# A 2-layer encoder trunk on one core: the input also comes transposed from the host, and the first norm drops its transposes

## The chip, the cores and the metric

The kernel runs on one core of a Trainium2 chip. A core has five engines, each working through its own list of instructions in order: TensorE (PE, matrix products, with PEld for its weight loads), VectorE (DVE), ScalarE (ACT), GpSimd (POOL) and SyncE (SP). SP, ACT and POOL can issue DMAs; 16 DMA engines carry them. The metric is the device time of one execution in microseconds (us), as the median of several runs. Time before: 2310.28 us (three runs, 2310.16 to 2310.79).

## What is computed

Two residual layers over 256 tokens of width 2048, in float32, then a final norm. Layer 0 mixes with a gated MLP and long convolutions, layer 1 with two kinds of attention. Each layer has a gated feed-forward part behind its mixer.

```python
for l in range(DEPTH):                        # DEPTH = 2
    h = rms_norm(x, norm_mix[l])
    p = h @ ab_w_in[i]                        # layer 0; cd_w_in in layer 1
    ...
    x = x + y @ w_out[l]
    x = x + conv_glu_ffn(rms_norm(x, norm_ffn[l]), ...)
return rms_norm(x, final_norm)
```

The change concerns the first `rms_norm` and the first products behind it. The norm's gain is applied to x in front of the product, the division by the root mean square behind it, per token, when the accumulator is read.

## The kernel before

Every product with a large weight matrix is a `gemm` (L172) over 512 output columns. It walks through *weight tiles* of 256 input features by 512 columns (`CK = 2` feature tiles of 128). A weight tile arrives as float32 in a buffer `raw` (512 KB, `N_RAW = 4` buffers, `issue_dma`, L120, on SP's queue), and is split into a high part `wh` by a cast on ACT (L131) and a low part `wl = raw - wh` by a subtraction on DVE (L134; `issue_split`, L126; `N_SPLIT = 4` buffers). The activations, features on the partitions, are split the same way into `hth` and `htl`. A product of two floats is then three matmuls of the parts (L184 to L186). With 2 feature tiles and 2 token tiles of 128 a weight tile is 12 matmuls of 512 columns. There are 768 weight tiles; below they are called c0, c1, ... and the stretch in which PE works on one is called tile 0, tile 1, ... The first `gemm` of layer 0 is tiles 0 to 7, the second 8 to 15.

`feed` (L137) issues the DMAs six weight tiles ahead and the splits two ahead, at high priority. The order of the instructions on each engine is chosen when the program is built, by a planner that takes what it holds to be ready, the higher priority first; `keep_in_program_order` and `issue_after` pin an order. Between two weight tiles `between` (L162) advances the side work: `soon` holds what a finished block needs next, `later` the mixers, which begin with the filter network of the long convolutions (`filt_mlp`, products at L470).

The head of the kernel: SP's queue loads x token-major in four blocks of 512 columns (`load_x`, L241), in turn with the first four weight tiles, and the gains. PE does 9 transposes of the identity (`WARM`, L922). `Norm.turn` (L289) transposes x on PE, 8 transposes a block (L296), ACT scales the result by the gain into `hth` (L301) and DVE makes `htl` (L304). Block 0 is turned ahead of the first product, the other three as the first pieces of `soon`, each between two weight tiles. Behind them ACT takes the squares of x for the mean (L286). Behind the last block of x a gate on POOL (L615) lets the constants of layer 0 go out on POOL's queue. Behind the first `gemm` come the root mean square (`finish`, L314) and the Gelu that reads the accumulators (L630).

Of the kernel before, what the change touches and what calls it, by code (L numbers as in the profile page):

```python
# [12 lines left out]
F32 = mybir.dt.float32  # L13
# [7 lines left out]
P = 128  # L21
# [26 lines left out]
WARM = 9  # L48
# [12 lines left out]
def trunk(ctx: ExitStack, tc: tile.TileContext, A, out, dbg=None):  # L61
# [24 lines left out]
    # ---------------------------------------------------------------- weights  # L86
# [59 lines left out]
    # Work beside the products: `soon` holds what a finished block needs next,  # L146
    # `later` the mixers; one piece of either goes between two weight tiles.
# [63 lines left out]
    class Parts:  # L211
        """A matrix [feature, token] in two parts, by feature tiles."""
# [25 lines left out]
    # -------------------------------------------------------------- constants  # L238
# [8 lines left out]
    with tc.high_priority():  # L247
        for n in range(4):
            load_x(n)
            if n == 0:  # L250
                nc.sync.dma_start(gains, A["gains"])
            issue_dma(st["dma"])
            st["dma"] += 1
# [10 lines left out]
    def rsqrt_to(dst, ssq, n, width):  # L264
        """dst = (ssq / n + EPS) ** -0.5"""
# [9 lines left out]

    class Norm:
        """Running sum of squares of the residual, block by block, and x * gain transposed."""
# [11 lines left out]
        def turn(self, n, halves=(0, 1), ordered=False):  # L289
            for j in halves:  # L290
                tp = tp_tile().rearrange("p (k t) -> p k t", k=2)
                tp = [tp[:, 0], tp_tile()[:, :T] if ordered else tp[:, 1]]
# [5 lines left out]
                for q in range(2):  # L298
                    kt = 4 * n + 2 * j + q
                    g = gains[:, self.gi, kt:kt + 1]  # L300
                    self.last = ACT.activation(hth[:, kt], tp[q], AF.Copy, scale=g)  # L301
                    if ordered:
                        tc.keep_in_program_order(self.last)
# [29 lines left out]
    def transposed(es):  # L333
        """Two PSUM tiles [feature, 2, token] from the token tiles [token, 512]."""
# [10 lines left out]
    def dwconv(es, cw, base, dst):  # L345
        """dst[:, f] (f of 4 feature tiles, tokens) = depthwise conv over tokens."""
# [11 lines left out]
    # ------------------------------------------------------------ out projection  # L358
# [17 lines left out]
    # -------------------------------------------------------------------- FFN  # L376
# [44 lines left out]
    # ---------------------------------------------------------------- layer 0  # L421
    def layer0(pre, norm):
        with ExitStack() as es_:
# [8 lines left out]
            mix = [mix_tile(i) for i in range(3)]  # L432
# [6 lines left out]
            # constants of the odd-frequency transform, tokens as (even, odd)  # L439
# [22 lines left out]
            def filt_mlp():  # L462
                """hs = [h; h'] and hd = [-h; h'], h' being h without its token 0."""
# [24 lines left out]
            def forward(ah, al, per):  # L488
                """Transforms of the even and the odd tokens: two tiles [freq, (cos, sin), channel]."""
# [14 lines left out]
            def filt_unit(half, order, kq, rn):  # L504
                """kq = K[f] and conj K[255 - f] for 512 channels, rn = 1 / (256 sum |k|)."""
# [35 lines left out]
            def long_conv(half, order, u, kq, rn, dst):  # L541
                """dst = (u conv k) / sum |k| + skip u, channels on the partitions."""
# [44 lines left out]
            # ---- gMLP  # L587
# [499 lines left out]
```

## Time and profile before

| | |
|---|---|
| time, median of 3 runs | 2310.28 us (2310.16 to 2310.79) |
| span of the profiled execution | 2309.2 us |
| PE busy | 2293.3 us, 99% of the span |
| DVE, ACT, POOL busy | 1437.6, 1191.6, 47.0 us |
| DMA | 418.42 MB, 181 GB/s on average |
| chain that ended last | PE 97% |

The profile's page gives, for one profiled execution, each engine's busy time, the costliest groups of instructions and the chain of work that ended last. Its trace can be asked for the instructions of a stretch in order of time (a *timeline*: start, duration, engine, line, operation, what it writes and reads, and in brackets how long the engine sat idle before it and what ended that), for the waits, for the DMAs from issue to landing, and for busy times by stretches. Durations of matmuls overlap, since they are pipelined; the distance from one start to the next is the time that one takes.

### The profile page before, as it was taken

The numbers are of one execution on the slowest core, as the hardware profiler recorded it, in microseconds if no ns is written. First come the engines' busy times: TensorE is split into PE (matmuls) and PEld (weight loads), VectorE is DVE, ScalarE is ACT, GpSimd is POOL, SyncE is SP. The second block draws the span as 40 slices with busy tenths as digits, with TensorE's granted clock in tenths as the row PEclk, the third lists the DMA queues.
The fourth block names the chain that finished last, engine by engine and source line by source line (L and its number), as shares of the span: only waits on it lengthen the run. The fifth ranks groups of instructions, "written<-read, shape, count | busy, mean of one in ns | idle before, by whom it ended". The sixth has DMA issues, their size and how long they took to land.

```text
span 2309.2 us, 28305 instructions
## 1 busy us (share of the span) xinstructions
PE 2293.3 (99%) x10733; PEld 1901.5 (82%) x10733; DVE 1437.6 (62%) x1816; ACT 1191.6 (52%) x1576; POOL 47.0 (2%) x85
## 2 busy tenths in 40 slices
PE   9999999999999999999999999999999999999998
PEld 7888888888888888888888888888888888888886
DVE  6677777666565456656556566766666644566654
ACT  6555545555553345555445545565555533555543
POOL 2000000000000000000001000000000000000000
PEclk9999999999999999999999999999999999999999
DMA  8554455566666666666666555456656566566664
GB/s 281 158 156 157 147 154 156 185 188 186 186 186 194 192 187 188 185 187 189 186 203 184 177 169 155 156 167 197 187 185 188 183 190 186 189 185 186 187 185 142
DMA packets 116649, 418.42 MB, mean 181 GB/s; under 512 B 13754, under 2 KB 13781, under 8 KB 116384
## 3 DMA queue, kind: packets, MB, share of 16 engines
q1 hardware_dynamic: 112688, 406.41, 57.3%
q0 software_dynamic: 3536, 9.68, 1.4%
q8 instruction: 84, 1.38, 0.2%
q10 hardware_dynamic: 288, 0.52, 0.1%
q14 instruction: 53, 0.43, 0.1%
HBM read 414.46 MB, written 2.10 MB: 180 GB/s over the span
## 4 chain that ended last, share of the span: by engine, by line
PE 97%; issue 1%; DVE 1%; ACT 1%; DMA 0%; SPq 0%; POOL 0%; POOLq 0%; DVEq 0%; ACTq 0%
PE acc L184 30%; PE acc L186 30%; PE acc L185 30%; PE tp L341 2%; PE tp L230 1%; PE tp L231 1%; PE tp L232 1%; PE tp L520 0%; DMA raw<-in_ab_w_in 0%; PE tp L296 0%; DVE wl L134 0%; ACT wh L131 0%; PE tp L729 0%; ACT junk L286 0%; PE tp L593 0%
## 5 line engine op out<-in xcount | busy, mean ns | idle before, releaser
L134 DVE TENSOR_TENSOR wl<-raw,wh 128x1024 fp32r<-128x1024 f32 x768 | 939.9, 1224 | 772.4 <-ACT wh L131 772.0
L131 ACT CAST wh<-raw 128x1024 fp32r<-128x1024 f32 x768 | 807.0, 1051 | 931.5 <-PE acc L186 824.7
L184 PE MATMUL acc<-wh,hth 128*128 128x512 f32 x2112 | 833.0, 395 | 1.7 <-ACT wh L131 1.7
L186 PE MATMUL acc<-wh,htl 128*128 128x512 f32 x2112 | 824.8, 391 | 0.6 <-DVE htl L304 0.6
L185 PE MATMUL acc<-wl,hth 128*128 128x512 f32 x2112 | 824.8, 391 | 0.0
L186 PEld LDWEIGHTS acc<-wh,htl 128*128 128x128 f32 x2112 | 397.0, 188 | 84.3 <-DVE htl L304 1.5
L184 PEld LDWEIGHTS acc<-wh,hth 128*128 128x128 f32 x2112 | 397.2, 188 | 82.3 <-ACT wh L131 2.1
L185 PEld LDWEIGHTS acc<-wl,hth 128*128 128x128 f32 x2112 | 397.2, 188 | 79.0 <-DVE wl L134 0.8
L184 PE MATMUL acc<-wh,gth 128*128 128x512 f32 x704 | 276.7, 393 | 0.0
L186 PE MATMUL acc<-wh,gtl 128*128 128x512 f32 x704 | 276.1, 392 | 0.0
L185 PE MATMUL acc<-wl,gth 128*128 128x512 f32 x704 | 276.1, 392 | 0.0
L186 PEld LDWEIGHTS acc<-wh,gtl 128*128 128x128 f32 x704 | 132.2, 188 | 29.9
L185 PEld LDWEIGHTS acc<-wl,gth 128*128 128x128 f32 x704 | 132.2, 188 | 29.6
L184 PEld LDWEIGHTS acc<-wh,gth 128*128 128x128 f32 x704 | 132.2, 188 | 29.4
L352 ACT ACTIVATE cv<-tp,cw 128x256 f32<-128x256 f32 x176 | 94.3, 560 | 68.0 <-DVE cv L355 68.0
L184 PE MATMUL acc<-wh,mh 128*128 128x512 f32 x256 | 102.3, 400 | 0.8 <-ACT mh L898 0.8
L185 PE MATMUL acc<-wl,mh 128*128 128x512 f32 x256 | 100.2, 391 | 0.0
L186 PE MATMUL acc<-wh,ml 128*128 128x512 f32 x256 | 99.9, 392 | 0.0
L329 ACT ACTIVATE e<-acc,rs 128x512 f32<-128x512 f32 x116 | 79.7, 687 | 18.4 <-PE acc L186 18.4
L353 DVE SCALAR_TENSOR_TENSOR cv<-tp,cw,cv 128x255 f32<-128x255 f32 x176 | 80.3, 477 | 10.7 <-ACT cv L352 10.7
L355 DVE SCALAR_TENSOR_TENSOR cv<-tp,cw,cv 128x255 f32<-128x255 f32 x176 | 80.4, 477 | 3.1
L184 PEld LDWEIGHTS acc<-wh,mh 128*128 128x128 f32 x256 | 48.2, 188 | 10.8 <-ACT mh L898 1.1
(227 smaller groups left out, 1341.2 us busy)
## 6 DMA issues: line engine op xcount, KB each, us to landing
raw<-in_ffn_up SPq DMA_DIRECT2D x352, 512.0 KB, 3.6
raw<-in_ffn_down SPq DMA_DIRECT2D x176, 512.0 KB, 3.6
raw<-in_cd_w_in SPq DMA_DIRECT2D x96, 512.0 KB, 3.6
raw<-in_ab_w_in SPq DMA_DIRECT2D x80, 512.0 KB, 3.6
raw<-in_w_out SPq DMA_DIRECT2D x64, 512.0 KB, 3.6
x_sb<-in_x SPq DMA_DIRECT2D x4, 512.0 KB, 8.2
uh<-in_decay POOLq DMA_DIRECT2D x8, 256.0 KB, 3.3
bias<-in_rpb_band POOLq DMA_DIRECT2D x32, 64.0 KB, 3.2
```

The lines of the kernel that those rows point to most:

```text
L131: cpy = ACT.copy(wh, r)
L134: DVE.tensor_tensor(wl, r, wh.bitcast(F32), ALU.subtract)
L184: PE.matmul(accs[t], lhsT=xh[:, ts_], rhs=wh[:, q], start=first, stop=False)
L185: PE.matmul(accs[t], lhsT=xh[:, ts_], rhs=wl[:, q], start=False, stop=False)
L186: mm = PE.matmul(accs[t], lhsT=xl[:, ts_], rhs=wh[:, q], start=False, stop=last)
L230: PE.matmul(o, lhsT=ah, rhs=bh, start=start, stop=False)
L231: PE.matmul(o, lhsT=ah, rhs=bl, start=False, stop=False)
L329: ACT.activation(e, accs[t], AF.Copy, scale=rs[:, t:t + 1])
L341: PE.transpose(tp[:, q, t * P:(t + 1) * P], es[t][:, f * P:(f + 1) * P], ident)
L352: ACT.activation(d, tp, AF.Identity, bias=w[:, 3:4], scale=w[:, 1:2])
L353: DVE.scalar_tensor_tensor(d[:, 1:T], tp[:, 0:T - 1], w[:, 0:1], d[:, 1:T], op0=ALU.mult, op1=ALU.add)
L355: DVE.scalar_tensor_tensor(d[:, 0:T - 1], tp[:, 1:T], w[:, 2:3], d[:, 0:T - 1], op0=ALU.mult, op1=ALU.add)
```

## The change

The host also hands over x transposed, as `xt`: four blocks, each with 4 feature tiles of 128 features by 256 tokens. `split_x` makes `hth` and `htl` for the first norm straight from `xt`, with the same two instructions per feature tile as before but from SBUF instead of PSUM, so PE's 32 transposes of x at the head go. Block 0 of `xt` comes in two halves on ACT's queue, behind the gains; blocks 1 to 3 on SP's queue behind weight tiles 2, 4 and 6. The first weight tile is loaded and split in two halves. On ACT the order of the head is pinned: feature tile 0, the two halves of c0, feature tile 1, c1, feature tiles 2 and 3. x itself, token-major, is loaded later, its four blocks behind weight tiles 7, 9, 11 and 12, and its squares and the root mean square are pieces of `soon` behind tiles 6, 8, 9 and 10. The Gelu of the first two `gemm`s becomes a piece of `soon` as well. The gate of the constants waits for block 2 of `xt`. The blocks of `xt` use the buffers of the mixers' results, which are handed out later than before. 16 transposes of the identity stand at the start instead of 9.

```diff
-WARM = 9
+WARM = 16
+XT_AFTER = {2: 1, 4: 2, 6: 3}
+X_AFTER = {7: 0, 9: 1, 11: 2, 12: 3}
...
     def issue_dma(i):
         w, k, c0 = chunks[i]
         r = wp.tile([P, CK, NB], F32, tag="raw", name=nm("raw"), bufs=N_RAW)
-        nc.sync.dma_start(r, w[k // CK, c0 // NB])
+        for c in range(CK if i == 0 else 1):
+            cs = slice(c, c + 1 if i == 0 else CK)
+            nc.sync.dma_start(r[:, cs], w[k // CK, c0 // NB][:, cs])
         raws[i] = r
+        if i in XT_AFTER:
+            nc.sync.dma_start(st["xt"][XT_AFTER[i]], A["xt"][XT_AFTER[i]])
+        if i in X_AFTER:
+            load_x(X_AFTER[i])
...
-        cpy = ACT.copy(wh, r)
-        if i < 2:
-            tc.keep_in_program_order(cpy)
-        DVE.tensor_tensor(wl, r, wh.bitcast(F32), ALU.subtract)
+        for c in range(CK if i == 0 else 1):
+            cs = slice(c, c + 1 if i == 0 else CK)
+            cpy = ACT.copy(wh[:, cs], r[:, cs])
+            if i < 2:
+                tc.keep_in_program_order(cpy)
+            DVE.tensor_tensor(wl[:, cs], r[:, cs], wh[:, cs].bitcast(F32), ALU.subtract)
...
+    def split_x(n, xt, ks):
+        for k in ks:
+            kt = 4 * n + k
+            g = gains[:, 0, kt:kt + 1]
+            hi = ACT.activation(hth[:, kt], xt[:, k], AF.Copy, scale=g)
+            if n == 0:
+                tc.keep_in_program_order(hi)
+            DVE.scalar_tensor_tensor(htl[:, kt], xt[:, k], g, hth[:, kt].bitcast(F32),
+                                     op0=ALU.mult, op1=ALU.subtract)
+            n0.h.wrote(kt)
+        return hi
...
-            mix = [mix_tile(i) for i in range(3)]
+            xt = [mt([P, 4, T], f"m{hl}{i}") for i in range(2) for hl in "hl"]
+            with tc.high_priority():
+                ACT.dma_start(gains, A["gains"])
+                for k in range(2):
+                    ACT.dma_start(xt[0][:, 2 * k:2 * k + 2], A["xt"][0, :, 2 * k:2 * k + 2])
+                st["xt"] = xt
+                for _ in range(5):
+                    issue_dma(st["dma"])
+                    st["dma"] += 1
+            begin(xt)
+            mix = [None] * 3
...
-            gate_op = POOL.tensor_copy(gate, x_sb[:, 0, D - 1:])
+            gate_op = POOL.tensor_copy(gate, xt[2][:, 3, T - 1:])
...
+            for n in range(2):
+                accs = gemm(pre.h.tiles(KT), w_in, 0, AW + n * NB)
+                soon.append(gelu_v(accs, n))
+            while soon:
+                between()
...
-    for half in range(2):
-        n0.turn(0, [half], True)
+    def begin(xt):
+        ACT.copy(nhalf[:, 8:], nhalf[:, :8])
+        warm = tp_tile()
+        for _ in range(WARM):
+            PE.transpose(warm[:, :P], ident, ident)
+        split_x(0, xt[0], [0])
         issue_split(st["split"])
         st["split"] += 1
+        split_x(0, xt[0], [1])
+        issue_split(st["split"])
+        st["split"] += 1
+        split_x(0, xt[0], [2, 3])
+
+        def run():
+            for n in range(1, 4):
+                split_x(n, xt[n], range(4))
+                yield
+            for n, wait in enumerate((3, 1, 3, 1)):
+                for _ in range(wait):
+                    yield
+                n0.squares(n)
+            n0.finish()
+            yield
+        soon.append(run())
```

## Rows read from the trace of the kernel before

**Rows 1.** The page, busy time, share of span and instructions of the engines.
```profile
PE 2293.3 (99%) x10733; PEld 1901.5 (82%) x10733; DVE 1437.6 (62%) x1816; ACT 1191.6 (52%) x1576; POOL 47.0 (2%) x85
```

**Rows 2.** PE's waits from 40 us on: us in total, times, longest.
```profile
PE acc L184 <- ACT mh L898: 0.8, 1, 0.8
```

**Rows 3.** By stretches: length, PE, PEld, DVE, ACT, POOL busy, PEclk, DMA share, GB/s.
```profile
8.63:13.62 4.99, 4.95 (x12) 3.46 (x13) 3.22 (x4) 1.73 (x3) 0.00 (x0) 1.00 1.04 399
13.62:14.41 0.79, 0.79 (x9) 0.78 (x8) 0.00 (x0) 0.71 (x1) 0.00 (x0) 1.00 1.03 410
...
18.06:22.33 4.27, 3.68 (x15) 2.13 (x14) 4.27 (x7) 3.60 (x7) 3.87 (x8) 1.00 0.83 277
...
25.97:28.69 2.72, 2.72 (x13) 2.25 (x12) 2.12 (x5) 2.31 (x5) 0.23 (x1) 1.00 1.04 337
...
31.50:37.67 6.17, 6.17 (x27) 4.61 (x26) 5.75 (x12) 6.06 (x13) 0.73 (x1) 1.00 1.02 393
```

**Rows 4.** PE's timeline at the head: start us, us, what, idle before.
```profile
1.41 2.18 PE L923 MATMUL tp<-ident 128*128 128x128 f32 x9 [1.41 <-POOL ident masks.py:199]
4.98 1.97 PE L296 MATMUL tp<-ident,x_sb 128*128 128x128 f32 x8 [1.39 <-DMA x_sb<-in_x]
8.63 1.22 PE L184 MATMUL acc<-wh,hth 128*128 128x512 f32 x2 [1.68 <-ACT wh L131]
...
10.91 0.63 PE L184 MATMUL acc<-wh,hth 128*128 128x512 f32 x1
11.33 0.63 PE L185 MATMUL acc<-wl,hth 128*128 128x512 f32 x1
...
20.60 0.50 PE L186 MATMUL acc<-wh,htl 128*128 128x512 f32 x1 [0.28 <-DVE htl L304]
...
38.43 0.70 PE L470 MATMUL tp<-zl,w 64*128 64x256 f32 x2 [0.60 <-ACT zl L481]
39.06 0.50 PE L184 MATMUL acc<-wh,hth 128*128 128x512 f32 x1
```

**Rows 5.** SP's timeline: the issues of x's second and third block.
```profile
2.21 0.43 SPq L242 DMA_DIRECT2D x_sb<-in_x  x1
...
3.19 0.65 SPq L242 DMA_DIRECT2D x_sb<-in_x  x1
```

**Rows 6.** The DMA lists of those two issues: KB each, us from issue to landing.
```profile
x_sb<-in_x SPq DMA_DIRECT2D x1, 512.0 KB, 7.3
...
x_sb<-in_x SPq DMA_DIRECT2D x1, 512.0 KB, 9.2
```

**Rows 7.** ACT's timeline at the head; nine casts (L131) stand from 7.53 to 30.22.
```profile
0.73 1.28 ACT L920 ACT_TABLE_LOAD   x1 [0.73 <-PEq L1076]
...
7.53 1.04 ACT L131 CAST wh<-raw 128x1024 fp32r<-128x1024 f32 x1 [0.93 <-DMA raw<-in_ab_w_in]
...
11.06 1.05 ACT L131 CAST wh<-raw 128x1024 fp32r<-128x1024 f32 x1 [1.74 <-DMA raw<-in_ab_w_in]
13.70 1.05 ACT L131 CAST wh<-raw 128x1024 fp32r<-128x1024 f32 x1 [1.59 <-DMA raw<-in_ab_w_in]
16.32 1.05 ACT L131 CAST wh<-raw 128x1024 fp32r<-128x1024 f32 x1 [1.58 <-DMA raw<-in_ab_w_in]
17.28 0.47 ACT L301 ACTIVATE hth<-tp,gains 128x256 fp32r<-128x256 f32 x1
17.64 1.03 ACT L131 CAST wh<-raw 128x1024 fp32r<-128x1024 f32 x1
...
30.22 1.03 ACT L131 CAST wh<-raw 128x1024 fp32r<-128x1024 f32 x1
```

**Rows 8.** DVE's timeline around the wait in tile 2.
```profile
18.94 1.21 DVE L134 TENSOR_TENSOR wl<-raw,wh 128x1024 fp32r<-128x1024 f32 x1
20.07 0.86 DVE L304 SCALAR_TENSOR_TENSOR htl<-tp,gains,hth 128x256 fp32r<-128x256 f32 x2
```

**Rows 9.** By stretches, as rows 3, behind the head.
```profile
40.00:45.00 5.00, 5.00 (x24) 4.13 (x23) 3.79 (x8) 4.95 (x9) 0.00 (x0) 1.00 0.42 130
```

More of the change, by code (lines that the diff above doesn't have):

```diff
@@ L246, in trunk @@
     gains = cp.tile([P, 4, KT], F32, tag="gains", name="gains")
[L247 to L253, printed above, removed]
     ident = cp.tile([P, P], F32, tag="ident", name="ident")
@@ L287, in squares, with turn @@
                                accum_out=self.ss[:, t, n:n + 1])
-        def turn(self, n, halves=(0, 1), ordered=False):
-            for j in halves:
+        def turn(self, n):
+            for j in range(2):
                 tp = tp_tile().rearrange("p (k t) -> p k t", k=2)
-                tp = [tp[:, 0], tp_tile()[:, :T] if ordered else tp[:, 1]]
+                tp = [tp[:, 0], tp[:, 1]]
                 for q in range(2):
@@ L300, in turn @@
                     g = gains[:, self.gi, kt:kt + 1]
-                    self.last = ACT.activation(hth[:, kt], tp[q], AF.Copy, scale=g)
-                    if ordered:
-                        tc.keep_in_program_order(self.last)
+                    ACT.activation(hth[:, kt], tp[q], AF.Copy, scale=g)
                     DVE.scalar_tensor_tensor(htl[:, kt], tp[q], g, hth[:, kt].bitcast(F32),
@@ L600, in spatial @@
                 for j, tp in enumerate(transposed([gu[:, t] for t in range(NT)])):
+                    if mix[n] is None:
+                        mix[n] = mix_tile(n)
                     split_to(mix[n].h[:, 2 * j:2 * j + 2], mix[n].l[:, 2 * j:2 * j + 2], tp)
@@ L623, in layer0, with gelu_v @@
             ssv = mt([P, NT, 2], "ssv")
-            for n in range(2):
-                accs = gemm(pre.h.tiles(KT), w_in, 0, AW + n * NB)
-                if n == 0:
-                    pre.finish()
+            def gelu_v(accs, n):
                 gv = mt([P, NT, NB], ("cx0", "cx1")[n])
@@ L675, in order_task @@
                 else:
-                    if half == 1:
-                        mix[3] = mix_tile(3)
-                    m = mix[2 + half]
+                    m = mix[2 + half] = mix_tile(2 + half)
                     split_to(m.h, m.l, d)
@@ L919, in trunk @@
     n0, n1, n2, n3, n4 = Norm(0), Norm(1), Norm(2), Norm(3), Norm(None)
-    ACT.copy(nhalf[:, 8:], nhalf[:, :8])
-    warm = tp_tile()
-    for _ in range(WARM):
-        PE.transpose(warm[:, :P], ident, ident)
-    for half in range(2):
-        n0.turn(0, [half], True)
+    def begin(xt):
[4 more added lines that the diff above has]
+        split_x(0, xt[0], [0])
         issue_split(st["split"])
         st["split"] += 1
-    def start():
-        for n in range(1, 4):
-            n0.turn(n)
+        split_x(0, xt[0], [1])
[11 more added lines that the diff above has]
+            n0.finish()
             yield
-        with tc.issue_after(n0.last.ins):
-            for n in range(4):
-                n0.squares(n)
-    soon.append(start())
+        soon.append(run())
     layer0(n0, n1)
@@ L1030, in _arrays @@
     a["x"] = i["x"][0]
+    a["xt"] = i["x"][0].T.reshape(4, 4, P, T).transpose(0, 2, 1, 3)
     a["gains"] = np.stack([col(i["norm_mix"][0]), col(i["norm_ffn"][0]),
```

## The prediction

> **What bounds the kernel now.** I read the busy times first: TensorE (PE) is busy 2293.3 of 2309.2 us [rows 1]. Then PE's waits: after 40 us the longest in all is 0.8 us, in layer 1 [rows 2]. So everything behind about 40 us is a rigid row of products, and a change at the head moves the end one for one, as far as it moves the first products and leaves the later ones covered. Third, the head, cut by weight tiles [rows 3]. A weight tile is 12 products; undisturbed it takes 2.72 us, 0.227 us a product. Tile 0 runs from 8.63 to 13.62, 4.99 us; then 8 transposes take 0.79 us, as two more groups of 8 do behind tiles 1 and 2; tile 1 starts at 14.41; tile 2 takes 4.27 us, 18.06 to 22.33; with its transposes behind it tile 3 starts at 23.12. Last, the timeline [rows 4]: why tile 0 is slow. Its products stand 0.42 us apart (10.91, 11.33), which for 512 columns is 1.2 GHz; from tile 1 on the spacing is that of the 2.4 GHz level. The granted-clock column reads 1.00 in both stretches, so here the spacing tells it, not the column. Before it PE had done transposes from 1.41 to 3.6 and from 5 to 7 us, with pauses between.
>
> **How bytes land now.** At the head one queue moves x and weights in turn, 512 KB each, and each lands behind the one before: x's first block 4.98, weight tile c0 7.53, second x 2.21+7.3=9.5, c1 11.06, third x 3.19+9.2=12.4, c2 13.70, c3 16.32 [rows 4 to 7]. So the first, second, ... sixth half megabyte is there at 5.0, 7.5, 9.5, 11.1, 12.4, 13.7. The 16 engines are busy at 1.04 of their span in tile 0 [rows 3]: no spare rate.
>
> **The change, part by part.** *Order of the bytes.* First half megabyte: half of the transposed block 0 (xt0) on ACT's queue and half of c0 on SP's; second: their other halves; then c1, c2, xt1, c3. I take the same landing times by position, whichever queue. The gains (32 KB) stand ahead of xt0: 0.1 us.
> The row shows that the engines, not the issue, limit the flow. The Trainium skill (DMA: Bandwidth & Descriptors, "Issuing engines are not separate DMA queues") says the same against the second queue: transfers issued from different engines share the 16 DMA engines and only issue time is saved. If instead the two queues really added up, c1 would land at the second position, 7.5, and PE's own pace would set tile 1 (10.0 to 11.2 us), up to 1.2 us better than my sum.
>
> *First product.* It needs k=0 of x, scaled (one ACTIVATE of 256 columns, 0.47) and the high part of half of c0, a cast of 512 columns: 1.04 for the whole tile, so between 0.52 and 1.04; I take 0.55, near half, since a 256-column ACTIVATE at 0.47 against 1.04 for 1024 shows some fixed part [rows 7]. 5.1+0.47+0.55 = 6.1 instead of 8.63: 2.5 us. ACT's three issues come before its table load; if the 1.28 us load [rows 7] came first, xt0 is 1.3 us later and the start 7.4, which tile 1 below would mostly swallow. The 16 warm-up transposes (9 took 2.18 us [rows 4], so 3.9 us, 1.4 to 5.3) end before the first product; they cost nothing.
>
> *Tile 0.* Six products of k=0 at 0.42: 6.1 to 8.65. k=1 needs the second half of c0 (7.5), its cast and one ACTIVATE behind it in ACT's pinned order: 7.5+0.55+0.47 = 8.5, covered. Six more: to 11.2 at the slow pace, 10.0 at the fast one. *Tile 1* needs c1 (9.5), its cast 1.05 and k=2 behind it 0.47: 11.0. So tile 1 starts at 11.2 at most and 11.0 at least, whatever the clock: 3.2 us sooner than 14.41.
>
> *Tile 1* pays the low parts: VectorE needs 1.22 for the tile's and 0.43 to 0.45 each for k=2 and k=3 [rows 8], that is 11.8, 12.2, 12.7. With products in the order written, the last wait is at 12.7 and seven products follow: end 14.4 (13.95 if other products fill in). Tile 2 started at 18.06, since a group of transposes (0.79) went between: 3.65 us sooner.
>
> *Tile 2.* Before, it lost 1.55 us, because ACT, which works strictly in order, stood at the cast of c3 until 16.32 while x's second block had long landed, and then took the cast of c4 behind k=4 [rows 7]; VectorE followed with wl, then htl at 20.07 to 20.9 [rows 8], and the product that needs it went at 20.60 [rows 4]. Now xt1 is there at 12.4, before c3. If ACT takes k=4 and k=5 when they are there (cast of c2 11.45 to 12.5, k=4 12.95, k=5 13.4, low parts 14.2 and 14.6), tile 2 runs 14.4 to 17.1: against 23.12 the gain is 6.0. If the cast of c3 (13.7 to 14.75) falls between k=4 and k=5, k=5 is done at 15.2, its low part behind wl at 16.4, and seven products later it is 18.0: gain 5.1. I take 5.5, between them.
>
> *Afterwards.* Tiles 3 to 7 need xt2 and xt3 (about 16.3 and 20) at 22 and 28 us: covered. The eight squares, now behind the last scaled tile on ACT, come between tiles 6 and 11. One wait of 0.60 us at the filter's second product (38.43, for ACT's sine behind its 1.28 us table load) [rows 4] is as likely to stay as to go: 0, range -0.6 to +0.8. First Gelu behind tile 11 instead of 7: the four accumulators are next needed behind tile 15, covered by 11 us of products. Draining `soon` behind tile 15 runs two filter steps early; their first product needs a weight load issued some two tiles before: 0, to +0.5. Moving the constants' gate from the last x block to xt2 shifts them by about one transfer, 1.3 us, while the filter's first product, behind tile 5 (31.4 now), comes 5.5 us earlier: 0, to +0.5, since ten us of other work lie between gate and product.
> *Token-major x*, 2 MB more, stands between weight tiles 7 and 13 on SP's queue. That queue already waits for free raw buffers, and c8's cast was done at 31.25 for use at 39.06 [rows 4, 7]; with PE 5.5 sooner and one more transfer ahead (1.3 us at 400 GB/s) 1 us of cover is left. From 40 us the DMA share falls to 0.42 [rows 9], so the rest is absorbed: 0.
>
> **Sum.** The profiled execution (2309.2 span) minus 5.5 is 2303.7; the median stands 1.1 above that span, so 2304.8.
>
> **The rivals.** *A cast again goes first (B).* The order on ACT is fixed when the program is built, and weight casts have the higher priority. If c3's cast stands ahead of k=4 as it did in the trace before, k=4 is done at 15.2 and its low part, behind wl, at 16.4; with one more cast, of c4, ahead or between, k=5's low part comes at 18.1. Tile 2 then ends between 18.7 and 20.0, the gain is 4.4 to 3.1, and the removed transposes are partly replaced by waiting for the same ACT: 2310.3-3.8 = 2306.5. For it: exactly this stands at 16.32 to 17.64 [rows 7]. Against: xt1 has no transposes to wait for and lands before c3.
> *The extra 2 MB starves the weights (C), slower.* From 26 to 38 us the engines are at 1.02 to 1.04 of their span while the constants load [rows 3]. If SP's queue gets half of 400 GB/s all that time, a weight tile takes 2.6 us against 2.73 us of products, no cover is regained, and the x blocks add 2.6 us each; 2.3 us are left of the cover after PE's gain, so 10.4-2.3 = 8.1 us of stalls: 2310.3-5.5+8.1 = 2312.9. It turns slower from 5.5 us of stalls, that is if three of the four transfers go at half rate. Against: the constants are 2.7 MB by their shapes and end with the first two, and the share of 0.42 follows [rows 9].
> *ACT freed (E).* No cast between (6.0), the 0.6 us at 38.43 gone, tile 0 at the fast pace or products filling tile 1's wait (0.4): 2310.3-7.0 = 2303.3.
>
> **How the numbers follow.** Forecast 0.48, B 0.38, C 0.06, E 0.08. What a measurement of this kernel can tell from no change is about 0.2%, 4.6 us, that is 2305.7. Faster by more: most of the forecast (0.40), a little of B (0.06), E: 0.54. Within: the rest of forecast and B, 0.40. Slower: C, 0.06. The range reaches from E's 2303.0 to B's lower gain and 1 us of other waits, 2308.0; outside are C and what lies past either end.
>
> **What would show it.** First product near 6.1; tile 1 near 11.2; tile 2 starting near 14.4 with k=4 right behind c2's cast (forecast) or behind c3's (B); no transposes between tiles; tile 8 starting near 33.5 without a wait on its cast (else C). A c1 landing later than 9.5, or another wait behind tile 3, would make it wrong.

## The result and the profile after

The changed kernel takes 2325.01 us (2324.47 to 2325.63), the kernel before 2310.28 (2309.92 to 2310.79): ratio 1.0063, interval 1.0051 to 1.0075. The forecast was 2304.8 (2303.0 to 2308.0); the change is 14.7 us slower. The profiled execution has a span of 2322.9 us against 2309.2, 13.7 more. In all that follows, "line" means the line of the kernel whose view is shown; products are L194 to L196 after the change and L197 to L201 in most experiments.

PE's waits over the whole run, the longest first (us in total, times, longest). They answer to rows 2:

```profile
PE acc L194 <- ACT hth L284: 10.3, 1, 10.3
PE acc L194 <- ACT wh L141: 10.1, 1, 10.1
```

There are two, and no other is over 1.4 us: one for a cast of weights, one for a scaled tile of x. PE's timeline says where (start, us, what, idle before), beside rows 4:

```profile
14.91 1.22 PE L194 MATMUL acc<-wh,hth 128*128 128x512 f32 x2 [10.08 <-ACT wh L141]
...
37.85 0.79 PE L194 MATMUL acc<-wh,hth 128*128 128x512 f32 x1 [10.27 <-ACT hth L284]
...
41.43 0.63 PE L196 MATMUL acc<-wh,htl 128*128 128x512 f32 x1
41.86 0.46 PE L194 MATMUL acc<-wh,hth 128*128 128x512 f32 x1
42.16 0.39 PE L195 MATMUL acc<-wl,hth 128*128 128x512 f32 x1
```

The first product comes at 14.91 instead of 8.63 (forecast 6.1), and in front of tile 4 PE stands from 27.43 to 37.85. Between the two, tiles 0 to 3 take 12.52 us instead of 17.34 (8.63 to 25.97): there the change does what it was forecast to do, no transposes and no wait in tile 2. SP's timeline shows what SP issued instead of the written order (start, time over all of the row's issues, what):

```profile
0.74 0.38 SPq L130 DMA_DIRECT2D ml<-in_xt  x1
1.18 1.99 SPq L252 DMA_DIRECT2D x_sb<-in_x  x4
4.83 4.02 SPq L127 DMA_DIRECT2D raw<-in_ab_w_in  x4
8.89 0.43 SPq L130 DMA_DIRECT2D ml<-in_xt  x1
9.37 21.37 SPq L127 DMA_DIRECT2D raw<-in_ab_w_in  x9
30.79 0.43 SPq L130 DMA_DIRECT2D mh<-in_xt  x1
```

In the source c0 and c1 come first, each further block of xt stands behind a weight tile, and token-major x behind c7 to c12. In the program xt3 is first (tile `ml` of the first row), then all four blocks of token-major x, then c0 in its two halves, c1, c2, then xt1, c3 to c11, and xt2 (`mh`) at 30.79 behind c11. The loads of xt and x go into tiles of their own and wait for nothing, so the planner was free to move them. The weight loads wait for a raw buffer, and xt2 stands behind them.

ACT shows both prices:

```profile
7.53 1.69 ACT L284 ACTIVATE hth<-ml,gains 128x256 fp32r<-128x256 f32 x4
9.12 0.61 ACT L302 ACTIVATE junk<-x_sb 128x512 bf16<-128x512 f32 x1
...
14.26 0.60 ACT L141 CAST wh<-raw 128x512 fp32r<-128x512 f32 x1
...
37.29 1.71 ACT L284 ACTIVATE hth<-mh,gains 128x256 fp32r<-128x256 f32 x4 [8.17 <-DMA mh<-in_xt]
```

The first cast of c0 comes at 14.26, behind the scaling of xt3 (7.53) and seven of the eight squares (9.12 to 14.16), which the planner had put ahead of it on ACT. c0's first half, issued at 4.83, landed only 7.8 us later, so ACT's order costs about 1.6 of the delay and SP's the rest. The second price is the 8.17 us for xt2.

The windows around the second wait, columns as in rows 3:

```profile
27.43:37.85 10.42, 0.15 (x1) 0.00 (x0) 1.43 (x3) 1.60 (x3) 0.53 (x2) 0.71 0.64 221
37.85:41.86 4.01, 4.00 (x9) 3.14 (x10) 1.67 (x4) 1.15 (x3) 4.01 (x8) 0.50 0.27 61
```

After ten idle microseconds the granted clock stands at 0.50, that is 1.2 GHz, and nine products in a row stand 0.43 us apart; from 41.86 on they stand 0.23 apart, the spacing of 2.4 GHz. That is another 2 us on top of the wait.

The account, by the starts of weight tiles against those of before: tile 0 is 6.28 late; tiles 0 to 3 win 4.82 back; the wait adds 10.42, so that tile 4 is 11.88 late; the slow products cost 2.07, and 0.45 come back in front of tile 8, where PE waits 0.2 us for the filter instead of 0.60 [rows 4]. Tile 8 is 13.5 late, and that distance stays: 13.7 at the end.

### The profile page after: what moved, and what is told of

Same layout as the page of the kernel before. It is cut to its first block, busy times and chain, and to the rows that moved or that the text cites. A ratio compares the mean times of both kernels' runs of the same rounds, so it can differ in the third digit from the quotient of the medians.

```text
span 2322.9 us, 28277 instructions
## 1 busy us (share of the span) xinstructions
PE 2290.9 (99%) x10708; PEld 1899.8 (82%) x10708; DVE 1437.8 (62%) x1817; ACT 1192.2 (51%) x1577; POOL 46.5 (2%) x85
## 4 chain that ended last, share of the span: by engine, by line
PE 98%; DMA 1%; ACT 1%; issue 0%; DVE 0%; POOLq 0%; POOL 0%; ACTq 0%; DVEq 0%; SPq 0%
PE acc L194 30%; PE acc L195 30%; PE acc L196 30%; PE tp L355 2%; PE tp L240 1%; PE tp L241 1%; PE tp L242 1%; PE tp L546 1%; DMA mh<-in_xt 1%; PE tp L312 0%; PE tp L759 0%; ACT wh L141 0%; ACT junk L302 0%; DMA raw<-in_ab_w_in 0%; PE tp L591 0%
## 5 line engine op out<-in xcount | busy, mean ns | idle before, releaser
L144 DVE TENSOR_TENSOR wl<-raw,wh 128x1024 fp32r<-128x1024 f32 (+1 forms) x769 | 939.9, 1223 | 778.8 <-ACT wh L141 778.2
L141 ACT CAST wh<-raw 128x1024 fp32r<-128x1024 f32 (+1 forms) x769 | 807.0, 1050 | 941.0 <-PE acc L196 839.9
L194 PE MATMUL acc<-wh,hth 128*128 128x512 f32 x2112 | 832.9, 395 | 20.4 <-ACT hth L284 10.3
L196 PE MATMUL acc<-wh,htl 128*128 128x512 f32 x2112 | 824.8, 391 | 0.0
L194 PEld LDWEIGHTS acc<-wh,hth 128*128 128x128 f32 x2112 | 397.7, 188 | 101.3 <-ACT hth L284 10.7
L196 PEld LDWEIGHTS acc<-wh,htl 128*128 128x128 f32 x2112 | 397.2, 188 | 82.8
L194 PE MATMUL acc<-wh,gth 128*128 128x512 f32 x704 | 276.6, 393 | 0.0
L196 PE MATMUL acc<-wh,gtl 128*128 128x512 f32 x704 | 276.1, 392 | 0.0
L196 PEld LDWEIGHTS acc<-wh,gtl 128*128 128x128 f32 x704 | 132.1, 188 | 29.7
L194 PEld LDWEIGHTS acc<-wh,gth 128*128 128x128 f32 x704 | 132.2, 188 | 29.6
L194 PE MATMUL acc<-wh,mh 128*128 128x512 f32 x256 | 102.4, 400 | 0.8 <-ACT mh L928 0.8
L196 PE MATMUL acc<-wh,ml 128*128 128x512 f32 x256 | 100.1, 392 | 0.0
L194 PEld LDWEIGHTS acc<-wh,mh 128*128 128x128 f32 x256 | 48.2, 188 | 11.0 <-ACT mh L928 1.1
```

The source lines that it names most:

```text
L141: cpy = ACT.copy(wh[:, cs], r[:, cs])
L144: DVE.tensor_tensor(wl[:, cs], r[:, cs], wh[:, cs].bitcast(F32), ALU.subtract)
L194: PE.matmul(accs[t], lhsT=xh[:, ts_], rhs=wh[:, q], start=first, stop=False)
L196: mm = PE.matmul(accs[t], lhsT=xl[:, ts_], rhs=wh[:, q], start=False, stop=last)
```

## The experiments

### What makes it slower: the order on SP's queue

Three kernels mark some of SP's loads with `keep_in_program_order`, so that the planner does not take them ahead of what the source has before them; nothing else is changed. The first marks c1 to c19, all blocks of xt on SP's queue and all of x, and SP's timeline then has the written order:

```diff
-            nc.sync.dma_start(r[:, cs], w[k // CK, c0 // NB][:, cs])
+            d = nc.sync.dma_start(r[:, cs], w[k // CK, c0 // NB][:, cs])
+            if 0 < i < 20:
+                tc.keep_in_program_order(d)
...
-            nc.sync.dma_start(st["xt"][XT_AFTER[i]], A["xt"][XT_AFTER[i]])
+            tc.keep_in_program_order(
+                nc.sync.dma_start(st["xt"][XT_AFTER[i]], A["xt"][XT_AFTER[i]]))
...
-        nc.sync.dma_start(
+        d = nc.sync.dma_start(
             x_sb[:, :, n * NB:(n + 1) * NB],
             A["x"][:, n * NB:(n + 1) * NB].rearrange("(t p) c -> p t c", p=P))
+        tc.keep_in_program_order(d)
```

The second marks only c5's load, which the source has behind xt2 (`if i == 5:` in the first hunk, the others left out); the third only the loads of x (the last hunk alone).

All loads held:

> The changed kernel with one thing added: every load on SP's queue among weight tiles 0 to 19, xt and x is pinned behind the one written ahead of it, so the queue carries the order that the change's text names (c0, c1, c2, xt1, c3, c4, xt2, c5, c6, xt3, c7, x0, c8, c9, x1, ...). Theory: the loss is the order in which the loads go out, nothing else; then the first product comes at 6 to 7 us, no wait of PE at the head is above 1.5 us, and the time is 2304 to 2306.5 us. Rival 1: the 2 MB more starve the weights wherever they stand; then PE waits for casts from tile 8 on and the time stays above 2311 us. Rival 2: ACT's order (squares ahead of casts) is the cause by itself; then the squares, which the planner may still put ahead, keep the first product above 10 us.

Only c5 held behind xt2:

> The changed kernel with one load pinned: weight tile c5 behind xt2, so that xt2 goes out behind c4 instead of behind c11; x and xt3 stay at the head of the queue. Theory (two separate losses): the wait of 10.3 us ahead of tile 4 and the slow products behind it (about 2 us) go, the first product stays at 14.9 us: 2325.0-12.4 = 2312.6, between 2311.5 and 2314 us. Rival (the bytes of x at the head are what makes everything late, xt2 too): the wait ahead of tile 4 shrinks by less than half, above 2318 us.

Only token-major x held behind its weight tiles:

> The changed kernel with only the four loads of x pinned behind their weight tiles; xt3 stays first on SP's queue and xt2 stays late. Theory: first product at 8 to 9.5 us (c0 behind xt3 and xt0, a megabyte, instead of three), xt2 still goes out only when weight tile 7 has been split, and now x blocks stand ahead of it as well, so the wait ahead of tile 4 stays at 8 to 12 us; the time is 2317 to 2321 us. Rival (the loads of x are the whole loss): below 2312 us.

Measured: 2312.03 with all held (ratio 1.0006, interval 0.9997 to 1.0016), 2314.54 with xt2 alone (1.0018, 1.0008 to 1.0027), 2325.97 with x alone (1.0065, 1.0050 to 1.0080). PE's waits over 1 us, first of the second kernel, then of the third:

```profile
PE acc L196 <- ACT wh L143: 10.1, 1, 10.1
PE tp L498 <- ACT zl L509: 1.5, 1, 1.5
```

```profile
PE acc L194 <- ACT hth L285: 12.3, 1, 12.3
PE acc L194 <- ACT wh L141: 8.2, 1, 8.2
```

Each of the last two removes the wait it was made for and keeps the other: with xt2 in place the second wait is gone and the first product still comes at 15.17; with x in place the first product comes at 8.19, and xt2, still behind c11, stops PE for 12.3 us. With both, 13.5 of the 14.7 us above the kernel before are gone. So the order on SP's queue makes the change slower, shown by undoing it in parts.

All three expectations missed. The first kernel has the number of its first rival (above 2311), but no wait for a weight cast behind the start, which that rival had. The second lies 0.5 us above its range, with a wait of 1.5 us for the filter. The third was expected at 2317 to 2321: tile 3 came 3.9 us sooner than after the change, but xt2, now behind three blocks of x as well, landed at 34.58 instead of 37.27, so that the wait grew by 2 us.

But 2312 is not 2305. The starts of weight tiles by PE's timelines tell where it goes (us; in brackets against the kernel before):

| tile | before | after | all loads held | constants later | and split | no warm-up |
|---|---|---|---|---|---|---|
| 0 | 8.63 | 14.91 (+6.3) | 7.35 (-1.3) | 7.57 (-1.1) | 7.23 (-1.4) | 7.45 (-1.2) |
| 1 | 14.41 | 19.25 (+4.8) | 14.00 (-0.4) | 15.16 (+0.8) | 14.58 (+0.2) | 12.75 (-1.7) |
| 2 | 18.06 | 21.98 (+3.9) | 16.73 (-1.3) | 17.88 (-0.2) | 17.32 (-0.7) | 15.49 (-2.6) |
| 3 | 23.12 | 24.70 (+1.6) | 19.45 (-3.7) | 20.60 (-2.5) | 20.04 (-3.1) | 18.21 (-4.9) |
| 4 | 25.97 | 37.85 (+11.9) | 22.17 (-3.8) | 23.32 (-2.7) | 22.76 (-3.2) | 20.93 (-5.0) |
| 8 | 39.06 | 52.56 (+13.5) | 35.67 (-3.4) | 35.96 (-3.1) | 35.40 (-3.7) | 33.64 (-5.4) |
| 13 | 56.31 | 69.81 (+13.5) | 55.58 (-0.7) | 53.21 (-3.1) | 52.65 (-3.7) | 50.89 (-5.4) |
| 14 | 60.68 | 74.18 (+13.5) | 61.54 (+0.9) | 60.15 (-0.5) | 57.02 (-3.7) | 55.26 (-5.4) |

(The last three columns are runs further below.) With all loads held the head wins 3.8 us up to tile 4 (the forecast had 5.5), and loses it between tiles 12 and 14. Two things are in this column. First, inside tile 0:

```profile
9.95 0.63 PE L199 MATMUL acc<-wh,htl 128*128 128x512 f32 x1
10.38 2.39 PE L959 MATMUL tp<-ident 128*128 128x128 f32 x16
12.53 0.48 PE L197 MATMUL acc<-wh,hth 128*128 128x512 f32 x1
```

The 16 warm-up transposes, which depend on nothing but the identity, were put behind the sixth product and take 2.15 us there (10.38 to 12.53). Second, behind tile 11, on POOL and ACT (rs is the reciprocal root mean square of the first norm):

```profile
45.25 1.57 POOL L275 TENSOR_TENSOR rs<-rsq,nhalf 128x2 f32<-128x2 f32 x1 [15.63 <-DVE rsq L274]
```

```profile
44.57 1.28 ACT L659 ACT_TABLE_LOAD   x1
46.86 0.69 ACT L659 ACTIVATE cx<-acc,rs 128x512 f32<-128x512 f32 x1 [1.01 <-POOL rs L275]
...
49.01 0.61 ACT L248 CAST zh<-uv 128x512 fp32r<-128x512 f32 x1
```

The last block of x landed at about 41, rs came at 46.8, and the Gelu that waits for it stands on ACT ahead of the filter's cast `zh`. Between tiles 12 and 13 PE waited three times for the filter, 0.24, 0.34 and 0.81 us, and behind the last of them the next eight products went 0.43 us apart; the granted clock of that stretch was 0.59:

```profile
24.00:42.00 18.00, 16.99 (x73) 12.96 (x72) 10.26 (x18) 10.35 (x20) 2.58 (x5) 1.00 1.05 393
...
55.00:59.00 4.00, 3.86 (x13) 3.12 (x13) 2.56 (x5) 0.59 (x1) 0.00 (x0) 0.59 0.81 229
```

The first of these rows is the suspect for the lateness: the DMA engines are busy without a gap up to 42 us at 393 GB/s. Over the first 40 us, first this kernel, then the kernel before:

```profile
0.00:40.00 40.00, 31.63 (x135) 24.94 (x136) 23.67 (x39) 25.95 (x44) 10.34 (x24) 1.00 0.98 364
0.00:40.00 40.00, 34.29 (x145) 25.98 (x146) 23.21 (x38) 27.55 (x49) 10.93 (x25) 1.00 0.91 321
```

That is 364 GB/s x 40 = 14.6 MB against 321 x 40 = 12.8 MB.

### Is it the bytes, the Gelu, or the warm-up?

Four kernels start from the one with all loads held. The first issues 2 MB of constants behind rs instead of behind xt2's landing:

```diff
-            n0.finish()
+            with tc.issue_after(n0.finish().ins):
+                st["late"]()
```

Here `st["late"]` issues wst, bst, avg, hcw, skip, gh and gl, which are taken out of `load_constants`.

> The queue order of the loads as in the run with SP's loads in written order (2312.0), and 2 MB of constants that are needed only behind tile 16 (spatial weights, their bias, the gain, the conv weights, the two back transforms) are issued behind the first norm's rs instead of ahead of it. Theory (the bytes are late: x and the filter's operands queue behind the constants, rs is late, and the Gelu that waits for it stands ahead of the filter's casts on ACT): the 3.8 us gained by tile 4 live past tile 14, which starts 3 to 4 us ahead of the kernel before, with no clock drop at 55 us; time 2308.3 (2307.0 to 2309.5). Rival (the order on ACT alone, whatever the bytes): tile 14 again 0.5 to 1 us late and 2311 to 2313.

Measured: 2309.1 (ratio 0.9995, 0.9985 to 1.0004). The number lies in the theory's range, but the way there is neither side's. Up to tile 13 the theory holds: ACT does not wait once for x, and tile 13 starts 3.1 us ahead of the kernel before. Then PE waits in a new place, and tile 14 is only 0.5 us ahead:

```profile
PE tp L554 <- DMA ul<-in_filt_w: 2.3, 1, 2.3
```

The operand of the second filter, 128 KB, was now issued behind the 2 MB. The edit moved the queue from one user to another.

The second puts the first Gelu three steps later:

```diff
             def gelu_v(accs, n):
+                for _ in range(3 if n == 0 else 0):
+                    yield
```

> Loads in written order, the constants where the change has them, and only the first Gelu put three steps of the side work later. Theory (ACT stands at the Gelu that waits for rs, with the filter's casts behind it): the waits of PE at tiles 12 to 14 go, tile 14 starts 3 to 4 us ahead of the kernel before, and the time is 2308.3 (2307 to 2309.5). Rival (the filter's own operands are late, for they come behind the constants in POOL's queue): the waits stay, 2311 to 2313.

Measured: 2311.65 (1.0006, 0.9996 to 1.0015). This decides nothing: the edit changed the order of tracing, but on ACT the Gelu stood where it was, at 47.31 behind rs and ahead of `zh` at 49.46, and PE still waited for the filter, 2.0 and 0.8 us the longest.

The third holds the warm-up ahead of the first product:

```diff
-            PE.transpose(warm[:, :P], ident, ident)
+            tc.keep_in_program_order(PE.transpose(warm[:, :P], ident, ident))
...
-                PE.matmul(accs[t], lhsT=xh[:, ts_], rhs=wh[:, q], start=first, stop=False)
+                mm = PE.matmul(accs[t], lhsT=xh[:, ts_], rhs=wh[:, q], start=first, stop=False)
+                if st["use"] == 1:
+                    tc.keep_in_program_order(mm)
```

> Loads in written order, and the 16 warm-up transposes held ahead of the first product instead of inside tile 0 (2.15 us there). Theory (the head is limited by bytes until about 42 us): tile 1 starts at 12.0 to 12.6 instead of 14.0, but the gain is taken back by tile 14 by longer waits, 2311 to 2312.5. Rival (PE's products are the limit and what is late keeps its distance): the 1.5 to 2 us reach the end, 2310 to 2310.5.

Measured: 2317.58 (1.0031, 1.0020 to 1.0042), worse than both expectations. The head did as it should: tile 1 at 12.11, tile 4 at 20.31, 5.7 us ahead of before, the forecast's size. Then tile 8 came 4.4 us late. PE's wait, and ACT's:

```profile
PE tp L502 <- ACT zl L513: 10.2, 1, 10.2
```

```profile
ACT junk L308 <- DMA x_sb<-in_x: 10.5, 3, 5.5
```

ACT stood 10.5 us at the squares (`junk`) for blocks of x that had not landed, and behind them stood two weight casts and the sine `zl` of the filter's first step. The forecast had the squares "behind the last scaled tile on ACT", and gave them no price.

The fourth is the first and the third together, and drains `soon` behind tile 15 without running the filter along:

```diff
             while soon:
-                between()
+                step(soon)
```

> Loads in written order, the constants behind rs, the warm-up ahead of the first product, and the side work's queue drained behind tile 15 without running the filter ahead. Theory: the gain of the constants (3.7) and of the warm-up (1.5 to 2) add up to 2306.5 (2305.5 to 2308.0), and tile 16 loses nothing against tile 15 of the kernel before. Rival (bytes still limit, so the warm-up's gain is swallowed): 2308 to 2309.5; rival (order on ACT): 2311 and more.

Measured: 2312.21 (1.0007, 0.9998 to 1.0017). A miss, in the range of the rival that names ACT's order. The gain of 5.9 at tile 4 is lost again at tile 8 (wait for `zl` 4.3 us, and 2.3 more in slow products behind it); ACT stood 4.4 us for x. The draining was told apart here: tile 16 lost nothing against tile 15, where the kernels that run the filter along lose 1.6. But those get 1.8 back at tile 38, so that it moves nothing in the end, which is what the forecast had (0, to +0.5).

### ACT standing for x, or the bytes themselves?

Three kernels start from the one with the warm-up held. In the first, x is issued from POOL's queue, behind the first four small constants and ahead of all others; in the second, in addition, 0.6 MB of the constants go behind rs and 1.5 MB behind the gain's rs at tile 16 (a second `issue_after`, as above):

```diff
-        nc.sync.dma_start(
+        nc.gpsimd.dma_start(
             x_sb[:, :, n * NB:(n + 1) * NB],
...
-X_AFTER = {7: 0, 9: 1, 11: 2, 12: 3}
+X_AFTER = {}
```

> As the run with the warm-up held ahead of the first product (2317.6), but token-major x is issued from POOL's queue behind the first four small constants instead of from SP's behind weight tiles 7 to 12; the other constants follow it. Theory (ACT works strictly in order and stands at the squares for x, with the filter's sine and the weight casts behind them): x has landed when ACT comes to the squares, the 10.2 us wait at tile 8 goes or shrinks to under 2 us, and the time is 2305 to 2309. Rival (not the place of x but the sum of the bytes, so that the weight tiles themselves come late): PE waits for casts whose raw tile has just landed, and it stays above 2311.

> As the last one, and of the constants only what the filter needs early stays ahead of rs; 0.6 MB go behind rs, 1.5 MB (spatial weights and back transforms) behind the gain's rs at tile 16. Theory: neither x nor the second filter's operand is late, the 5.5 us gained at the head (tile 4 at 20.3) live to the end: 2304.9 (2304.0 to 2306.5). Rival (bytes): 2308 and more.

The third leaves the squares out:

```diff
-                n0.squares(n)
+            DVE.memset(n0.ss, 512.0)
```

> As the run with the warm-up held ahead of the first product (2317.6), loads and constants unchanged, but the squares of the first norm are left out (a constant stands in for their sum). Theory (ACT stands at the squares for x): the 10.2 us wait at tile 8 goes and the time is 2305 to 2308, though the same bytes are loaded. Rival (bytes): casts wait for their raw tiles instead, tile 8 still starts late, 2311 or more.

Measured: 2313.88 (1.0013, 1.0003 to 1.0022), 2313.84 (1.0012, 1.0002 to 1.0022) and 2312.73 (1.0007, 0.9998 to 1.0016). All three miss the theory. With x on POOL's queue ACT still stood 4.4 and 4.2 us at the squares, which came earlier on ACT along with x, and PE 5.7 and 5.4 us for `zl`. In the one without squares the rival came true. Up to 60 us, ACT's waits for weight tiles, the longest of them in ACT's timeline, and then the windows:

```profile
ACT wh L144 <- DMA raw<-in_ab_w_in: 9.4, 4, 4.6
...
33.88 1.04 ACT L144 CAST wh<-raw 128x1024 fp32r<-128x1024 f32 x1 [4.63 <-DMA raw<-in_ab_w_in]
```

```profile
24.00:32.00 8.00, 8.00 (x35) 5.93 (x33) 4.25 (x8) 2.10 (x2) 1.31 (x2) 1.00 1.07 400
32.00:40.00 8.00, 3.54 (x9) 2.26 (x8) 3.74 (x8) 6.06 (x7) 0.00 (x0) 0.70 1.05 399
```

With no square left to stand at, ACT stood 9.4 us for weight tiles, at 400 GB/s, and PE was stopped 4.5 us at tile 8 all the same. So late bytes do it without the squares: PE 5.6 us sooner and 2 MB more (2 MB at 400 GB/s are 5.2 us), and c10, issued at 22.89, lands at 33.78. The squares on ACT made it worse (10.2 against 4.5 us). But ACT's order has its part here too. Tile 8's own weights had been cast at 24.74; what PE waited for was the filter's sine, whose operand was there at 32.7 and which stood on ACT behind the cast of c10. This run does not tell the two apart.

One more kernel held ACT's order by hand, with x on SP's queue and the 2.1 MB of constants late:

```diff
-            if i < 2:
+            if i < 2 or 5 < i < 16:
                 tc.keep_in_program_order(cpy)
...
-            for n, wait in enumerate((3, 1, 3, 1)):
+            for n, wait in enumerate((3, 1, 1, 1)):
...
-                ACT.activation(junk_tile(), x_sb[:, t, n * NB:(n + 1) * NB], AF.Square,
+                sq = ACT.activation(junk_tile(), x_sb[:, t, n * NB:(n + 1) * NB], AF.Square,
...
+                if self.gi == 0:
+                    tc.keep_in_program_order(sq)
```

> Loads in written order on SP's queue (x behind weight tiles 7, 9, 11, 12), warm-up ahead of the first product, 2.1 MB of the constants behind rs and behind tile 16, and on ACT the squares held behind the weight casts 8 to 11. Theory (two causes, each enough: the bytes that must land by 40 us, and ACT standing at the squares for x): with both removed tile 8 starts at 33.2 to 33.6 and tile 14 at 55.0 to 55.8, 5 to 5.7 us ahead of the kernel before, and the time is 2305.3 (2304.3 to 2307). Rival (PE still meets a late operand, of the filter or of a weight tile): a wait of over 1 us between 30 and 60 us, and the slow products behind it: 2308 or more.

Measured: 2316.94 (1.0029, 1.0019 to 1.0039). A miss. ACT no longer stood for x, but now the planner had set the filter's two sines ahead of marked casts:

```profile
ACT zl L521 <- DVE uv L519: 6.0, 1, 6.0
ACT ko L540 <- PE tp L247: 5.3, 1, 5.3
ACT hs L521 <- DVE uv L519: 5.2, 1, 5.2
```

ACT stood 6.0 and 5.2 us for operands of the filter, with casts behind them whose weight tiles had landed (c7 at 20.4, cast at 29.4). Here the fixed order only moved the place where ACT stands.

### Does the forecast's gain exist at all?

The next two kernels have the constants split in the same way, so that the second filter's operand is no longer behind them:

```diff
+            with tc.issue_after(n0.finish().ins):
+                st["late"]()
...
-            rsqrt_to(rsv, sv, AW, NT)
+            with tc.issue_after(rsqrt_to(rsv, sv, AW, NT).ins):
+                load_last()
```

Here `st["late"]` issues avg, bst, hcw and skip, and `load_last` wst, gh and gl. The first kernel has nothing else beside all loads held; the second has the warm-up held too, and the filter two tiles later (`range(7)` for `range(5)` in `filt_mlp`).

> Loads in written order; 0.6 MB of constants behind rs, 1.5 MB behind the gain's rs at tile 16, so that the second filter's operand no longer queues behind them as in the run with all of them behind rs (2309.1, which lost 2.6 us there at tile 14). Theory: the 3.1 us that run held up to tile 13 reach the end: tile 14 at 57.6, 2307.6 (2306.8 to 2308.8). Rival (another late operand takes its place): tile 14 at 59.5 or later, 2309.5 or more.

> The same, with the 16 warm-up transposes ahead of the first product, and the filter's side work two weight tiles later. Theory: tile 4 starts at 20.2 and tile 14 5 to 5.8 us ahead of the kernel before, the forecast's gain reaches the end: 2305.3 (2304.4 to 2307.5). Rival (bytes or ACT's order still stop PE between 30 and 60 us): a wait of over 1 us there, 2308 or more.

Measured: 2307.84 (0.9988, 0.9979 to 0.9997) and 2311.44 (1.0002, 0.9993 to 1.0012). The first is as expected and beats both kernels. All of PE's waits in it, and its windows:

```profile
PE acc L197 <- ACT wh L144: 7.2, 1, 7.2
PE acc L197 <- ACT mh L940: 0.9, 1, 0.9
PE tp L570 <- DVE ha L563: 0.4, 1, 0.4
PE tp L506 <- ACT zl L517: 0.2, 1, 0.2
```

```profile
24.00:32.00 8.00, 8.00 (x36) 6.05 (x35) 5.42 (x9) 4.88 (x12) 0.00 (x0) 1.00 1.04 395
32.00:40.00 8.00, 7.85 (x34) 5.97 (x33) 6.25 (x13) 7.14 (x13) 0.00 (x0) 1.00 0.76 257
```

Behind the start (7.2) nothing stops PE for over 1 us, and from 32 us on the DMA engines have room again, where with the constants in place they were full up to 42. The second is a miss and went wrong in ACT's order once more: ACT stood 3.9 us for x, the first Gelu stood ahead of the sine, which came at 41.61, and PE waited 4.3 us for it, with slow products behind.

The last kernel is the better of these two without the warm-up; ACT's order up to the filter's first sine stays as it was.

```diff
-        warm = tp_tile()
-        for _ in range(WARM):
-            PE.transpose(warm[:, :P], ident, ident)
```

> As the run that reached 2307.8 (loads in written order, 2.1 MB of constants later), without any warm-up transposes. Theory: tile 0's twelve products stand 0.43 us apart, tile 1 starts at 12.3 to 12.8 instead of 14.6, and tile 14 is 4.5 to 5.8 us ahead of the kernel before: 2305.9 (2305.0 to 2306.8). Rival (the filter's sine on ACT is not earlier than 34.7 us): PE waits 1.5 to 2.2 us for it at tile 8 and nothing is won against that run: 2307.5 to 2309.

Measured: 2306.38 (0.9982, 0.9973 to 0.9991), the fastest of all here, 4.6 us under the kernel before. PE's timeline and PE's waits:

```profile
7.45 0.80 PE L197 MATMUL acc<-wh,hth 128*128 128x512 f32 x1 [7.45 <-ACT wh L144]
...
8.77 0.63 PE L199 MATMUL acc<-wh,htl 128*128 128x512 f32 x1
9.20 0.63 PE L197 MATMUL acc<-wh,hth 128*128 128x512 f32 x1
...
11.76 0.63 PE L197 MATMUL acc<-wh,hth 128*128 128x512 f32 x1
12.19 0.50 PE L198 MATMUL acc<-wl,hth 128*128 128x512 f32 x1
12.52 0.39 PE L199 MATMUL acc<-wh,htl 128*128 128x512 f32 x1
12.75 0.40 PE L197 MATMUL acc<-wh,hth 128*128 128x512 f32 x1
```

```profile
PE acc L197 <- ACT wh L144: 7.5, 1, 7.5
PE acc L197 <- ACT mh L940: 0.8, 1, 0.8
...
```

From tile 8 to tile 15 it is 5.4 us ahead of the kernel before, at 600 us 5.0, at the end of the span 4.9. So the gain that the forecast summed, 5.5, is there and reaches the end, less about 0.6 us that go between 270 and 390 us and that were not followed (the changed kernel loses 0.4 there too). This kernel has three things that the change does not have, and each has a step of its own in the runs: the loads in the written order (2325.0 to 2312.0), 2.1 MB of constants out of the first 40 us (to 2307.8), and no warm-up inside tile 0 (to 2306.4; the intervals of the last two overlap, but the trace keeps 1.8 us from tile 4 on). They are not enough by themselves. Three kernels with the order held, 2 MB of constants later and the warm-up ahead of the first product came out at 2312.21, 2316.94 and 2311.44, as ACT stood there for x or for the filter. In the last two kernels ACT's order fits the landings; it came from the planner and was not set.

## Why the prediction was wrong, step by step

*What bounds the kernel* held. PE is a rigid row behind the head: the 13.5 us by which tile 8 was late are 13.7 at the end, and the 3.7 and 5.4 of the better kernels arrive as 3.1 and 4.9.

*Order of the bytes* is the step that failed, and it alone makes the sign. It took the written order of the loads for the order on SP's queue. That held for the kernel before, where SP's loads stood as written [rows 5], and the prediction did think of the planner, but only for ACT's casts (rival B). A load into a tile of its own is an instruction without a dependency, and after the change the planner moved such loads. The sign was settled there: 14.7 us slower as the change stands, and with the order held 1.2, which can't be told from no change.

*First product* at 6.1: 7.35 with all loads held (6.93 to 7.57 in the others with the order held). xt0's first half, issued at 1.2 behind the gains, was there at 5.8 to 6.4 instead of 5.1, 6.2 in the run with all loads held; its scaling (0.5) and the cast of half a weight tile (0.6) took what was estimated (0.47 and 0.55). The term was short by 1.2 us there, nearly all of it in the landing. Tile 0 took the slow pace for most of its products, as allowed for, and tile 1 started at 11.6 to 12.9 where no transposes stood inside, against 11.2.

*The 16 warm-up transposes "cost nothing"* was right for the change as it stands, where they run from 1.41 to 4.83 and the first product comes at 14.91. It was wrong, in the same way as the order of the bytes, once all loads were held: without a dependency they were put behind the sixth product, 2.15 us. Leaving them out won 1.8 us at tile 4 (20.93 against 22.76).

*Tiles 1 to 3* were right with the order held. Tile 2 lost nothing to waiting, scaled tiles of xt1 came between the casts in time, and tile 3 started up to 6.0 us ahead of 23.12 (17.11 in the run with the filter later). Rival B did not happen in any kernel of the table.

*Token-major x "absorbed: 0"* is the second step that failed, a term mis-sized by what the first would have won. It looked for room behind 40 us [rows 9], and room is there; but the weights of tiles 8 to 12 and the filter's operands are needed before 40 us by a PE that runs 5.5 us sooner, and up to there the engines had little left already before the change (0.91 of their span from 0 to 40 us, 1.02 to 1.04 in four of the five rows of [rows 3]). 2 MB at 400 GB/s are 5.2 us. With the order held, 3.8 us won at tile 4 were 0.9 lost at tile 14. This is rival C by its place, at a chance of 0.06; its mechanism was put down as weights alone. In the runs it had three faces: late weights (9.4 us on ACT without the squares), ACT at the squares for x (10.5), and the Gelu for rs with the filter's cast behind it (three waits of 0.2 to 0.8 us and eight slow products). Against C the prediction had said that the constants "end with the first two" transfers. In the run with all loads held the first two blocks of x land at 22.2 and 29.2, the last constant at 36.9, close to the third block (37.9), and rs and the filter hang on what lands last.

*The transfers themselves.* For c1's landing the prediction had 9.5 if one flow is shared, and 7.5 if the two queues add up. Measured was a place between: in the run with the warm-up held c1's cast waited for its tile until 8.78, in the one without warm-up it started at 8.27 without a wait. The rate was 358 to 407 GB/s between 8 and 16 us in the runs with the order held, no more than the 399 and 410 that one queue moved before [rows 3]; so in rate the two queues did not add up, and why c1 was still sooner than 9.5 was not tried. The Trainium skill (DMA: Bandwidth & Descriptors, "Issuing engines are not separate DMA queues") says that transfers started by different engines run on the same 16 DMA engines; the rates agree with it.

*Draining `soon`, the gate, the Gelu at tile 11*: the draining cost 1.6 us at tile 16 and came back at tile 38, net 0 as forecast. The gate opened at 14.6 to 16.0 where the order was held (15.07 before); in the change as it stands it opened at 37.33, since it waits for xt2. The Gelu of tile 11 was free in the kernels at 2309.1, 2307.8 and 2306.4, where rs was there at 41.1 to 43.4. With all loads held it stood for rs (46.8) ahead of the filter's cast; in the run with the filter later it stood ahead of the filter's sine, though rs was there at 38.7.

## What to carry to other kernels

When a change moves loads, ask for each what its instruction depends on: one that waits for nothing stands where the planner likes, ahead of what is urgent or behind what waits for buffers, and the source's order is no promise unless it is held. Cost added bytes not against the room in the whole run but against the stretch before the first user that must not be late, and with the pace that the change itself would give. And where a strictly ordered engine serves both an early chain (casts) and a late one (squares, Gelu), a late landing costs at every instruction behind the one that waits: give the bytes their place first, and look at the engine's order after that.

## What the runs showed of the hardware

A stop of PE was paid twice, by the wait and by slow products behind it. After 10.42 us of idleness nine products stood 0.43 us apart at a granted clock of 0.50; after 10.2 us in the run with the warm-up held five did; after 4.5 us in the run without squares nine; and after a wait of 0.81 us behind a dozen short filter products, in the run with all loads held, the next eight, at 0.59 between 55 and 59 us. In the kernel before, a wait of 0.60 [rows 4] had no such tail.

The warm-up changed little. With 16 transposes from 1.41 to 5.1 and the first product at 7.16 (the first run with the warm-up held), the granted clock was 0.92 from 7.16 to 8.80, where the third and fourth product stood 0.34 and 0.24 behind the one ahead; then it was 0.52 up to 12.10, and the spacing of 0.43 ended at 11.8. In the other kernels with the warm-up ahead it ended between 10.2 and 12.9. Without any transposes and the first product at 7.45 it ended at 12.2.

SP's issue of a load could itself stop for the landing of another. After the change the issue of c0's first half waited 1.6 us for the gains to land, though neither has to do with the other's data; ahead of it stood five loads from SP and three from ACT. In the run with all loads held it was the sixth load of SP (c3), again behind five and three, that waited for the gains, 0.8 us. So the four blocks of x that stood in front cost c0 not only their bytes but also the issue.
